# Add and GELU of two 1024 x 4096 arrays: one DMA queue, x kept in place, the additions on GpSimd, temporaries in PSUM

## The chip, the cores and the metric

The kernel runs on one core of a Trainium2 chip. The metric is the device time of one execution in microseconds (us). Before the change the median of three runs is 132.72 us (132.6 to 132.73). A profile of one execution, taken by the hardware profiler, goes with it; all times inside the kernel are from that one execution and count from the start of its span.

The engines in the profile are DVE (VectorE), ACT (ScalarE), POOL (GpSimd) and SP (SyncE), which here only issues transfers. SPq and POOLq are the instruction queues of SP and POOL. PE, the matrix engine, is not used.

## The reference

```
x, y: float32 [1024, 4096]
z = x + y
out = 0.5 * z * (1 + tanh(sqrt(2/pi) * (z + 0.044715 * z**3)))      # float32
```

Every element is independent of the others. 33.55 MB are read and 16.78 MB written.

## The kernel before

Each of the 128 partitions holds 8 whole rows of the arrays, that is 32768 consecutive floats or 128 KB of HBM. The kernel walks along these 32768 columns in 20 tiles: 15 of 2048 columns (8 KB per partition, 1 MB per transfer), and then a tail of 1024, 512, 256, 128 and 128 columns. Within a transfer the pieces of two neighbouring partitions lie 128 KB apart in HBM.

A tile goes through seven steps. `do_load` (L67, L68) issues two loads on SP's queue, x into a tile `a` and y into a tile `b`. `do_add` (L75) forms z = a + b on DVE. `do_sq` (L81) writes w = (sqrt_k3 * z)^2 on ACT. `do_stt` (L90) makes w = (w + k1) * z on DVE, which is the argument of the tanh. `do_ti` runs Tanh (L100) and then Identity with scale 0.5 and bias 0.5 (L105) on ACT. `do_mul_store` multiplies z by w on DVE (L116) and issues the store on POOL's queue (L117). So DVE has three passes over the data and ACT three.

All tiles lie in SBUF: six buffers each for `a` and `b`, five each for `z` and `w`. The order of the work is written out as a software pipeline, and each engine executes its instructions in the order in which they are written:

```
for t in range(C + 4):
    do_load(t); do_ti(t - 3); do_add(t - 1); do_stt(t - 2); do_sq(t - 1); do_mul_store(t - 3)
```

Waits between engines, and between a transfer and its users, are put in by the framework from the tiles that an instruction reads and writes.

Of the kernel before, what the change touches and what calls it, by code (L numbers as in the profile page):

```python
# [1 line left out]

# [1 line left out]

# [4 lines left out]


@with_exitstack
def kernel(
    ctx: ExitStack,
    tc: tile.TileContext,
    x: bass.AP,
    y: bass.AP,
    out: bass.AP,
):
    nc = tc.nc  # L20
    P = nc.NUM_PARTITIONS
    fp32 = mybir.dt.float32

    N, D = x.shape
    assert N % P == 0
    rows_per_part = N // P

    k1 = math.sqrt(2.0 / math.pi)
    k3 = k1 * 0.044715
    sqrt_k3 = math.sqrt(k3)  # L30

    xv = x.rearrange("(p n) d -> p (n d)", p=P)
    yv = y.rearrange("(p n) d -> p (n d)", p=P)
    ov = out.rearrange("(p n) d -> p (n d)", p=P)

    total_free = rows_per_part * D
    FMAX = 2048

    tail = [1024, 512, 256, 128, 128]
    nbody = (total_free - sum(tail)) // FMAX  # L40
    assert sum(tail) + nbody * FMAX == total_free
    sizes = [FMAX] * nbody + tail
    offsets = []
    off = 0
    for F in sizes:
        offsets.append(off)
        off += F
    C = len(sizes)

    in_pool = ctx.enter_context(tc.tile_pool(name="inputs", bufs=6))  # L50
    chain_pool = ctx.enter_context(tc.tile_pool(name="chain", bufs=5))
    consts = ctx.enter_context(tc.tile_pool(name="consts", bufs=1))

    half = consts.tile([P, 1], fp32, tag="half")
    nc.vector.memset(half, 0.5)  # L55

    a_t: list = [None] * C
    b_t: list = [None] * C
    z_t: list = [None] * C
    w_t: list = [None] * C  # L60

    def do_load(c):
        F = sizes[c]
        sl = slice(offsets[c], offsets[c] + F)
        a = in_pool.tile([P, F], fp32, tag="a")
        b = in_pool.tile([P, F], fp32, tag="b")
        nc.sync.dma_start(out=a, in_=xv[:, sl])  # L67
        nc.sync.dma_start(out=b, in_=yv[:, sl])  # L68
        a_t[c] = a
        b_t[c] = b  # L70

    def do_add(c):
        F = sizes[c]
        z = chain_pool.tile([P, F], fp32, tag="z")
        nc.vector.tensor_add(out=z, in0=a_t[c], in1=b_t[c])  # L75
        z_t[c] = z

    def do_sq(c):
        F = sizes[c]
        w = chain_pool.tile([P, F], fp32, tag="w")  # L80
        nc.scalar.activation(  # L81
            out=w,
            in_=z_t[c],
            func=mybir.ActivationFunctionType.Square,
            scale=sqrt_k3,
        )
        w_t[c] = w

    def do_stt(c):
        nc.vector.scalar_tensor_tensor(  # L90
            out=w_t[c],
            in0=w_t[c],
            scalar=k1,
            in1=z_t[c],
            op0=mybir.AluOpType.add,
            op1=mybir.AluOpType.mult,
        )

    def do_ti(c):
        nc.scalar.activation(  # L100
            out=w_t[c],
            in_=w_t[c],
            func=mybir.ActivationFunctionType.Tanh,
        )
        nc.scalar.activation(  # L105
            out=w_t[c],
            in_=w_t[c],
            func=mybir.ActivationFunctionType.Identity,
            scale=0.5,
            bias=half,  # L110
        )

    def do_mul_store(c):
        F = sizes[c]
        sl = slice(offsets[c], offsets[c] + F)
        nc.vector.tensor_mul(out=w_t[c], in0=z_t[c], in1=w_t[c])  # L116
        nc.gpsimd.dma_start(out=ov[:, sl], in_=w_t[c])  # L117

    for t in range(C + 4):
        if 0 <= t < C:  # L120
            do_load(t)
        if 0 <= t - 3 < C:
            do_ti(t - 3)
        if 0 <= t - 1 < C:
            do_add(t - 1)
        if 0 <= t - 2 < C:
            do_stt(t - 2)
        if 0 <= t - 1 < C:
            do_sq(t - 1)
        if 0 <= t - 3 < C:  # L130
            do_mul_store(t - 3)


# [1 line left out]
_INS = ['x', 'y']  # L135
_OUTS = [((1024, 4096), 'float32')]


# [23 lines left out]
```

## Time and profile before

| | before |
|---|---|
| median of 3 runs | 132.72 us |
| span of the profiled execution | 130.8 us (the median lies 1.9 us above it) |
| DVE busy | 107.8 us, 82% of the span, 61 instructions |
| ACT busy | 96.0 us, 73%, 61 instructions |
| POOL busy | 11.0 us, 8%, 24 instructions, nearly all of it issuing stores |
| read / written | 33.55 MB / 16.78 MB, 385 GB/s over the span |

How to read the lines that follow. The page cuts the span into 40 equal slices of 3.27 us; a digit is the busy share of a slice in tenths, and 9 means 90% or more. The line "DMA" is the mean busy share of the core's 16 DMA engines and "GB/s" what they moved. In the view by stretches each row gives a stretch, its length, the busy time of each engine with the number of instructions begun, PE's granted clock, the DMA engines' share and the rate. In the view by groups a row gives line, engine, operation, output and inputs with their shapes, the count, the busy time in us and the mean of one in ns, and the idle time of the engine just before them with what ended it. In the view by order of time a row gives the start, the duration, engine, line and operation, and in brackets the idle time before it and who ended it.

### The profile page before, as it was taken

The page shows a single profiled execution, that of the slowest core. Times are in us where ns is not written, and L with a number is a line of the kernel's source. Part 1 is how long each engine was busy: PE and PEld are TensorE (multiplying, and loading weights), DVE is VectorE, ACT ScalarE, POOL GpSimd, SP SyncE. Part 2 cuts the span into 40 slices and gives each one's busy share as a digit, 9 for nine tenths or more (in the row PEclk, how much of TensorE's full clock was granted, in tenths as well). Part 3 has the DMA queues.
Part 4 walks back from the last instruction along what each step waited for, and adds up shares of the span by engine and source line. Part 5 has one row for each costly group of instructions (what it writes and reads, how often), then busy time and mean ns, then how long its engine had stood idle before and what let it go on. Part 6 is the DMA issues. An engine that isn't in the chain of part 4 may idle for free.

```text
span 130.8 us, 306 instructions
## 1 busy us (share of the span) xinstructions
DVE 107.8 (82%) x61; ACT 96.0 (73%) x61; POOL 11.0 (8%) x24
## 2 busy tenths in 40 slices
DVE  0053949999999999988959899998969799999930
ACT  3005492899998989895975979885975959899850
POOL 0000002001000000101010100101010100110341
DMA  4999999999999999999999999999999999717690
GB/s 140 428 421 431 431 416 428 341 423 416 439 426 418 436 429 418 436 428 418 436 426 421 436 423 423 434 426 421 436 426 421 417 414 389 310 53 321 271 342 29
DMA packets 8258, 50.35 MB, mean 385 GB/s; under 512 B 960, under 2 KB 1728, under 8 KB 2496
## 3 DMA queue, kind: packets, MB, share of 16 engines
q1 hardware_dynamic: 5760, 33.56, 62.1%
q0 software_dynamic: 2496, 16.78, 30.9%
q14 instruction: 2, 0.02, 0.0%
HBM read 33.55 MB, written 16.78 MB: 385 GB/s over the span
## 4 chain that ended last, share of the span: by engine, by line
DMA 44%; issue 43%; POOL 5%; DVE 3%; POOLq 1%; SPq 0%; DVEq 0%
DMA b<-in_y_dram 44%; POOL out_dram L117 5%; DVE w L90 2%; DVE w L116 2%; POOLq L157 0%; SPq L67 0%; POOLq L117 0%; DVE z L75 0%; DVEq L75 0%
## 5 line engine op out<-in xcount | busy, mean ns | idle before, releaser
L75 DVE TENSOR_TENSOR z<-a,b 128x2048 f32<-128x2048 f32 (+4 forms) x20 | 37.2, 1862 | 13.1 <-DMA b<-in_y_dram 13.1
L81 ACT ACTIVATE w<-z 128x2048 f32<-128x2048 f32 (+4 forms) x20 | 31.3, 1563 | 22.5 <-DVE z L75 22.1
L116 DVE TENSOR_TENSOR w<-z,w 128x2048 f32<-128x2048 f32 (+4 forms) x20 | 37.2, 1860 | 3.0 <-ACT w L105 3.0
L90 DVE SCALAR_TENSOR_TENSOR w<-w,z 128x2048 f32<-128x2048 f32 (+4 forms) x20 | 37.1, 1859 | 2.4 <-ACT w L81 2.4
L100 ACT ACTIVATE w<-w 128x2048 f32<-128x2048 f32 (+4 forms) x20 | 31.3, 1566 | 7.0 <-DVE w L90 6.9
L105 ACT ACTIVATE w<-w,half 128x2048 f32<-128x2048 f32 (+4 forms) x20 | 33.2, 1659 | 0.6
L117 POOL DMA_DIRECT2D out_dram<-w x20 | 10.8, 541 | 116.6 <-DVE w L116 114.7
L81 ACT ACT_TABLE_LOAD x1 | 1.3, 1283 | 0.7 <-PEq L146 0.7
L55 DVE MEMSET half<- 128x1 f32 x1 | 0.1, 59 | 0.8 <-PEq L146 0.8
L146 POOL MEMSET const-float32-0.0<- 128x1 f32 x1 | 0.1, 98 | 0.2 <-issue 0.2
L146 POOL MEMSET const-bfloat16-1.0<- 128x1 bf16 x1 | 0.1, 101 | 0.0
L146 POOL MEMSET const-float32-1.0<- 128x1 f32 x1 | 0.1, 98 | 0.0
L146 POOL MEMSET const-uint8-127<- 128x1 uint8 x1 | 0.1, 98 | 0.0
## 6 DMA issues: line engine op xcount, KB each, us to landing
a<-in_x_dram SPq DMA_DIRECT2D x15, 1024.0 KB, 27.4
b<-in_y_dram SPq DMA_DIRECT2D x15, 1024.0 KB, 28.2
out_dram<-w POOLq DMA_DIRECT2D x15, 1024.0 KB, 9.1
a<-in_x_dram SPq DMA_DIRECT2D x1, 512.0 KB, 28.7
b<-in_y_dram SPq DMA_DIRECT2D x1, 512.0 KB, 26.3
out_dram<-w POOLq DMA_DIRECT2D x1, 512.0 KB, 3.8
a<-in_x_dram SPq DMA_DIRECT2D x1, 256.0 KB, 23.2
b<-in_y_dram SPq DMA_DIRECT2D x1, 256.0 KB, 21.4
```

The lines of the kernel that those rows point to most:

```text
L55: nc.vector.memset(half, 0.5)
L75: nc.vector.tensor_add(out=z, in0=a_t[c], in1=b_t[c])
L81: nc.scalar.activation(out=w, in_=z_t[c], func=mybir.ActivationFunctionType.Square, scale=sqrt_k3,)
L90: nc.vector.scalar_tensor_tensor(out=w_t[c], in0=w_t[c], scalar=k1, in1=z_t[c], op0=mybir.AluOpType.add, op1=mybir.AluOpType.mult,)
L100: nc.scalar.activation(out=w_t[c], in_=w_t[c], func=mybir.ActivationFunctionType.Tanh,)
L105: nc.scalar.activation(out=w_t[c], in_=w_t[c], func=mybir.ActivationFunctionType.Identity, scale=0.5, bias=half,)
L116: nc.vector.tensor_mul(out=w_t[c], in0=z_t[c], in1=w_t[c])
L117: nc.gpsimd.dma_start(out=ov[:, sl], in_=w_t[c])
L146: nc = _bacc.Bacc("TRN2", target_bir_lowering=False, num_devices=1)
```

## The change

The tiling changes first. There are 13 tiles, of 1024, 1024, 2048, six times 4096, 2048, 1024, 512 and 512 columns; a partition still reads and writes its own 128 KB, in pieces of up to 16 KB. Each tile of x has an SBUF buffer of its own, so x is resident as a whole (128 KB per partition). y has four buffers of 4096 columns, shared by the smaller tiles of one block. z is written over x, and the result over z, so the store goes out of x's buffer.

Computation goes in 33 chunks of at most 1024 columns. `add` runs on GpSimd for chunks 2 to 30 and on DVE for the first two and the last two. The temporary `w` lies in PSUM, in four buffers of 1024 columns. The function is written with a sigmoid, z * sigmoid(c1 * z + c1 * 0.044715 * z^3), which is the same function; the Identity pass of ACT goes away. One Sigmoid on a single column (`one`) is executed first.

All loads and all stores are issued by SP, on one queue. `LEAD` = 8192 sets their order: the store of a tile stands behind the loads that reach 8192 columns beyond the tile's end. The order on each engine is written out in four lists (`sp`, `pool`, `dve`, `acts`); `needs` and the last loop only interleave these lists in program order so that each instruction is written after those it depends on.

```diff
-    tail = [1024, 512, 256, 128, 128]
-    sizes = [FMAX] * nbody + tail
+    LEAD = 8192
+    CH = 1024
+    YB = 4
+    sizes = [1024, 1024, 2048] + [D] * (NB - 2) + [2048, 1024, 512, 512]
+    starts = [sum(sizes[:t]) for t in range(len(sizes))]
+    T = len(sizes)
...
+    chunks = []
+    for t in range(T):
+        o = 0
+        while o < sizes[t]:
+            f = min(CH, sizes[t] - o)
+            chunks.append((t, o, f))
+            o += f
+    C = len(chunks)
+    last = {t: c for c, (t, _, _) in enumerate(chunks)}
+    by_pool = set(range(2, C - 2))
-    in_pool = ctx.enter_context(tc.tile_pool(name="inputs", bufs=6))
-    chain_pool = ctx.enter_context(tc.tile_pool(name="chain", bufs=5))
+    xpool = ctx.enter_context(tc.tile_pool(name="xz", bufs=1))
+    ypool = ctx.enter_context(tc.tile_pool(name="y", bufs=YB))
+    ppool = ctx.enter_context(
+        tc.tile_pool(name="w", bufs=4, space=bass.MemoryType.PSUM)
+    )
...
+    def load_x(t):
+        xt[t] = xpool.tile([P, sizes[t]], fp32, tag=f"x{t}", name=f"x{t}")
+        nc.sync.dma_start(out=xt[t], in_=hbm(x, t))
+    def load_y(t):
+        n, o = divmod(starts[t], D)
+        if o == 0:
+            yb[n] = ypool.tile([P, D], fp32, tag="y", name=f"y{n}")
+        yt[t] = yb[n][:, o : o + sizes[t]]
+        nc.sync.dma_start(out=yt[t], in_=hbm(y, t))
+    def store(t):
+        nc.sync.dma_start(out=hbm(out, t), in_=xt[t])
+    def z(c):
+        t, o, f = chunks[c]
+        return xt[t][:, o : o + f]
-        nc.vector.tensor_add(out=z, in0=a_t[c], in1=b_t[c])
+    def add(c):
+        t, o, f = chunks[c]
+        eng = nc.gpsimd if c in by_pool else nc.vector
+        eng.tensor_add(out=z(c), in0=z(c), in1=yt[t][:, o : o + f])
+    def sq(c):
+        f = chunks[c][2]
+        wt[c] = ppool.tile([P, CH], fp32, tag="w", name=f"w{c}")[:, :f]
+        nc.scalar.activation(out=wt[c], in_=z(c), func=act.Square, scale=root)
+    def stt(c):
         nc.vector.scalar_tensor_tensor(
-            out=w_t[c], in0=w_t[c], scalar=k1, in1=z_t[c], op0=add, op1=mult
+            out=wt[c], in0=wt[c], scalar=c1, in1=z(c), op0=alu.add, op1=alu.mult
         )
-        nc.scalar.activation(out=w_t[c], in_=w_t[c], func=Tanh)
-        nc.scalar.activation(out=w_t[c], in_=w_t[c], func=Identity, scale=0.5, bias=half)
+    def sig(c):
+        nc.scalar.activation(out=wt[c], in_=wt[c], func=act.Sigmoid)
-        nc.vector.tensor_mul(out=w_t[c], in0=z_t[c], in1=w_t[c])
-        nc.gpsimd.dma_start(out=ov[:, sl], in_=w_t[c])
+    def mul(c):
+        nc.vector.tensor_mul(out=z(c), in0=wt[c], in1=z(c))
...
+    for t in range(T):
+        sp += [(load_x, t), (load_y, t)]
+        while s < T and starts[s] + sizes[s] + LEAD <= starts[t] + sizes[t]:
+            sp.append((store, s))
+            s += 1
+    sp += [(store, t) for t in range(s, T)]
+    for c in range(C):
+        if c in by_pool:
+            pool.append((add, c))
+    for i in range(-3, C + 1):
+        if 0 <= i < C:
+            dve.append((stt, i))
+            acts.append((sig, i))
+        if 0 <= i - 1 < C:
+            dve.append((mul, i - 1))
+        if 0 <= i + 3 < C and i + 3 not in by_pool:
+            dve.append((add, i + 3))
+        if 0 <= i + 2 < C:
+            acts.append((sq, i + 2))
...
+        one = xpool.tile([P, 1], fp32, tag="one", name="one")
+        nc.vector.memset(one, 0.0)
+        nc.scalar.activation(out=one, in_=one, func=act.Sigmoid)
```

More of the change, by code (lines that the diff above doesn't have):

```diff
@@ L22 @@
     fp32 = mybir.dt.float32
+    act = mybir.ActivationFunctionType
+    alu = mybir.AluOpType
     N, D = x.shape
     assert N % P == 0
[L26 to L37, printed above, removed]
-    tail = [1024, 512, 256, 128, 128]
-    nbody = (total_free - sum(tail)) // FMAX
@@ L41 @@
-    assert sum(tail) + nbody * FMAX == total_free
-    sizes = [FMAX] * nbody + tail
[L43 to L48, printed above, removed]
-    in_pool = ctx.enter_context(tc.tile_pool(name="inputs", bufs=6))
-    chain_pool = ctx.enter_context(tc.tile_pool(name="chain", bufs=5))
[L52 to L85, printed above, removed]
-        )
[L87 to L131, printed above, removed]
+    NB = N // P
+    TOT = NB * D
+    c1 = 2.0 * math.sqrt(2.0 / math.pi)
+    root = math.sqrt(c1 * 0.044715)
+    LEAD = 8192
+    CH = 1024
@@ new lines, with hbm @@
+    YB = 4
+    sizes = [1024, 1024, 2048] + [D] * (NB - 2) + [2048, 1024, 512, 512]
+    assert sum(sizes) == TOT
+    starts = [sum(sizes[:t]) for t in range(len(sizes))]
+    T = len(sizes)
+    def hbm(ap, t):
+        v = ap.rearrange("(p n) d -> p (n d)", p=P)
+        return v[:, starts[t] : starts[t] + sizes[t]]
+    chunks = []
[5 more added lines that the diff above has]
+            o += f
@@ new lines, in sq @@
+    def sq(c):
[3 more added lines that the diff above has]
+    def stt(c):
+        nc.vector.scalar_tensor_tensor(
+            out=wt[c], in0=wt[c], scalar=c1, in1=z(c), op0=alu.add, op1=alu.mult
+        )
+    def sig(c):
+        nc.scalar.activation(out=wt[c], in_=wt[c], func=act.Sigmoid)
+    def mul(c):
+        nc.vector.tensor_mul(out=z(c), in0=wt[c], in1=z(c))
@@ new lines @@
+    needs = {
+        load_x: lambda t: [],
+        load_y: lambda t: [
+            (add, c)
+            for c, (i, _, _) in enumerate(chunks)
+            if starts[t] % D == 0 and starts[i] // D == starts[t] // D - YB
+        ],
+        add: lambda c: [(load_y, chunks[c][0]), (load_x, chunks[c][0])],
+        sq: lambda c: [(add, c)] + ([(mul, c - 4)] if c >= 4 else []),
+        stt: lambda c: [(sq, c)],
+        sig: lambda c: [(stt, c)],
+        mul: lambda c: [(sig, c)],
+        store: lambda t: [(mul, last[t])],
+    }
@@ new lines @@
+    queues = [sp, pool, acts, dve]
+    done = set()
+    with tc.manual_schedule():
+        one = xpool.tile([P, 1], fp32, tag="one", name="one")
+        nc.vector.memset(one, 0.0)
+        nc.scalar.activation(out=one, in_=one, func=act.Sigmoid)
+        while any(queues):
+            moved = False
+            for q in queues:
+                while q and all(n in done for n in needs[q[0][0]](q[0][1])):
+                    fn, arg = q.pop(0)
+                    fn(arg)
+                    done.add((fn, arg))
+                    moved = True
+                    if q is not sp:
+                        break
+            assert moved, [q[:1] for q in queues]
```

3 lines of the change are left out of this document (added).

## The prediction

> **What bounds the kernel now.** I read the page first: busy shares, the slices, the bytes.
>
> ```profile
> span 130.8 us, 306 instructions
> DVE 107.8 (82%) x61; ACT 96.0 (73%) x61; POOL 11.0 (8%) x24
> ...
> DMA  4999999999999999999999999999999999717690
> GB/s 140 428 421 431 431 416 428 341 423 416 439 426 418 436 429 418 436 428 418 436 426 421 436 423 423 434 426 421 436 426 421 417 414 389 310 53 321 271 342 29
> ...
> HBM read 33.55 MB, written 16.78 MB: 385 GB/s over the span
> ```
>
> The DMA digits are 9 from the second slice to the 34th, at about 425 GB/s, and then fall apart: one slice moves 53 GB/s. So the transfers set the pace for some 110 us, and in the last 20 us they wait for something. The next view is the busy time by stretch, with the DMA engines' share and rate.
>
> ```profile
> core 0: us, DVE busy (x) ACT busy (x) POOL busy (x), PEclk, DMA share, GB/s
> 0.00:2.00 2.00, 0.06 (x1) 1.27 (x1) 0.20 (x4) 1.00 0.17 37
> 2.00:3.00 1.00, 0.00 (x0) 0.02 (x1) 0.00 (x0) 1.00 0.84 270
> 3.00:4.00 1.00, 0.00 (x0) 0.00 (x0) 0.00 (x0) 1.00 1.03 426
> ...
> 60.00:80.00 20.00, 18.07 (x9) 14.48 (x9) 1.06 (x2) 1.00 1.01 428
> ...
> 110.00:114.00 4.00, 4.00 (x3) 3.73 (x3) 0.53 (x1) 1.00 0.79 295
> 114.00:118.00 4.00, 4.00 (x4) 3.56 (x2) 0.53 (x1) 1.00 0.28 113
> 118.00:122.00 4.00, 4.00 (x5) 3.68 (x6) 0.53 (x1) 1.00 0.61 250
> 122.00:126.00 4.00, 3.14 (x9) 3.06 (x9) 2.09 (x4) 1.00 0.93 374
> 126.00:131.00 5.00, 0.29 (x1) 0.69 (x2) 0.60 (x2) 1.00 0.34 120
> ```
>
> Loads and stores together run at 428 GB/s with a DMA share of 1.01: full. From 110 on DVE is busy for 12 us without a break while the DMA share drops to 0.28. DVE works off its backlog, and the stores wait. The order of instructions there:
>
> ```profile
> 116.87 0.53 POOL L117 DMA_DIRECT2D out_dram<-w  x1 [5.01 <-DVE w L116]
> ...
> 118.56 2.28 DVE L116 TENSOR_TENSOR w<-z,w 128x2048 f32<-128x2048 f32 x1
> ...
> 121.14 0.53 POOL L117 DMA_DIRECT2D out_dram<-w  x1 [3.74 <-DVE w L116]
> ```
>
> POOL, which issues the stores, waits 5.0 and 3.7 us for DVE's last multiplication. At 428 GB/s the 50.33 MB need 117.6 us; the span is 13.2 us longer. That is 2.2 us at the start (0 to 4 us move 74 + 270 + 426 KB = 0.77 MB, which is 1.8 us of full rate, so the stream starts in effect at 2.2), some 2 us after the last byte, and about 9 us of holes, nearly all behind 110.
>
> **The change, part by part.** The bytes stay, so the floor of 117.6 us stays. What can go is the holes.
>
> *Compute per 1024 columns.* The rows by shape:
>
> ```profile
> L75 DVE TENSOR_TENSOR z<-a,b 128x1024 f32<-128x1024 f32 x1 | 1.2, 1218 | 0.0
> L90 DVE SCALAR_TENSOR_TENSOR w<-w,z 128x1024 f32<-128x1024 f32 x1 | 1.2, 1218 | 0.0
> L81 ACT ACTIVATE w<-z 128x1024 f32<-128x1024 f32 x1 | 1.0, 1042 | 0.0
> L105 ACT ACTIVATE w<-w,half 128x1024 f32<-128x1024 f32 x1 | 1.1, 1132 | 0.0
> ...
> L75 DVE TENSOR_TENSOR z<-a,b 128x512 f32<-128x512 f32 x1 | 0.7, 686 | 0.0
> L81 ACT ACTIVATE w<-z 128x512 f32<-128x512 f32 x1 | 0.6, 612 | 0.0
> L81 ACT ACT_TABLE_LOAD x1 | 1.3, 1283 | 0.7 <-PEq L146 0.7
> ```
>
> The Identity pass goes (1.13 us per chunk), Sigmoid takes Tanh's place at Tanh's price, so ACT needs 2 x 1.04 = 2.08 us a chunk. Its one table load is called forth early by the activation on `one`, as now at 0.7 us, in the shade of the first load. DVE keeps two operations, 2 x 1.22 = 2.44 us a chunk, plus the adds of four chunks. Three streams of 512 KB a chunk are 1.573 MB, 3.67 us at 428 GB/s. Both engines have a third of their time to spare, so no backlog like that of now can build up.
>
> *PSUM operands.* The trace has none. The bound below is the SBUF row, 1.22; above, an operand at half speed makes 2.44 an operation, which would be 4.88 a chunk and more than the DMA's 3.67. I take 1.22 plus up to 0.1: nothing about a dense float row suggests a second pass over it. [...]
>
> *The add on GpSimd.* No row shows POOL computing a tile. Below stands DVE's row, 1.22. Above I put 3.66, DVE's price three times over, as for an engine that does its two reads and its write one after another. Between them I take 2.44, two reads after each other. Twenty-nine adds are 71 us beside a 118 us stream, 2.44 against 3.67 a chunk, so hidden. [...]
>
> *Stores on SP's queue.* POOL's 20 store issues go; SP now issues 26 loads and 13 stores in order. A store that waits for its multiplication holds every load behind it, and, as the next rows show, SP is held by another thing too.
>
> ```profile
> 4.17 0.45 SPq L68 DMA_DIRECT2D b<-in_y_dram  x1
> 5.60 0.33 SPq L67 DMA_DIRECT2D a<-in_x_dram  x1
> 8.06 0.33 SPq L68 DMA_DIRECT2D b<-in_y_dram  x1
> ```
>
> Twelve buffers are free, yet after eight issues the ninth waits, and the next come 2.46 us apart, one per landing: eight transfers may be outstanding on a queue. In the changed kernel eight are mostly 2 MB each, over 30 us of work, so that limit costs nothing. Does a store starve the stream? In the middle, store t-2 stands behind the loads of tile t. Its last multiplication comes on DVE after the next tile's first `stt`, and `sig` of that chunk comes on ACT after the next tile's first `sq`, so it waits for tile t-1 to land, then add, square, `stt`, multiplication: 1.0 + 2.44 + 1.04 + 1.22 + 1.22 = 6.9 us (the 1.0 is from the first tile: 2 MB from 2.2 on are through at 7.1, its add starts at 8.14). Behind tile t-1's landing the queue still holds store t-3 and tile t's loads, 14.7 us. That is 7.8 us of cover for one wait of SP. At the head, tile 3 lands at 22.8 (8.4 MB, 19.6 us, and 1.0 after 2.2), store 2 is ready 5.9 later at 28.7, and the loads ahead of it last until 31.6; stores 0 and 1 add 2.5. Cost nothing; without that cover it would be its lateness, microsecond for microsecond.
>
> *The tail.* Call E the moment the last load's data are through. Behind it stand stores 7 to 12, 6.3 MB or 14.7 us, under which the last chunks must be computed. Store 9 must start at E+9.8, so be issued by E+8.5 (first issue at 0.74, data from about 2.0: 1.3 us ahead). Tile 8's data are through at E-14.7 (store 6 and 4096 columns of loads follow), so by the prices above POOL's adds of it run from E-13.7 to E-3.9 and end for chunks 28 to 30 at E-1.5, 1.0 and 3.4; `stt` 28 is done at E+0.8 (1.04 + 1.22 later), and DVE runs without a gap from E+0.8 (mul 27, add 31, stt 29, mul 28, add 32, stt 30, mul 29: 5 x 1.22 + 2 x 0.69 = 7.5) to E+8.3. That is just in time; the last store is ready at E+12.2 against E+12.8. With up to 0.1 more for each PSUM operation a hole of up to 0.9 opens. I take 0.4.
>
> *Rate of the stream.* Every partition's rows lie 128 KB apart before and after; a row grows from 8 to 16 KB. Stores alone also run full, and the last bytes end like this:
>
> ```profile
> 118.00:119.00 1.00, 1.00 (x3) 1.00 (x3) 0.00 (x0) 1.00 1.03 426
> 119.00:120.00 1.00, 1.00 (x1) 1.00 (x2) 0.00 (x0) 1.00 1.05 426
> ...
> 127.00:128.00 1.00, 0.05 (x1) 0.00 (x0) 0.54 (x1) 1.00 0.56 193
> 128.00:129.00 1.00, 0.00 (x0) 0.00 (x0) 0.00 (x0) 1.00 0.19 66
> ```
>
> Loads alone 426 (3 to 4 us), both 428, stores alone 426: one queue in order should keep 428. Bounds: 421 (the poorer full slices), 119.5 us, and 436 (the better ones), 115.4 us. After the last byte, between 128.2 and 129, the span lasts 1.8 to 2.6 us; I take 2.3.
>
> **Sum.** 2.2 + 117.6 + 0.4 + 2.3 = 122.5 us of span. The median of the runs, 132.72, is 1.9 above the profiled span of 130.8, so 124.4 us, 8.3 less than before.
>
> **The rivals.**
>
> 1. *A hole in the tail.* If the add costs 3.0, POOL ends chunk 30 at E+7.3 instead of 3.4 (seven adds from E-13.7), store 9 is ready at E+10.8, 2.3 late, and later ones with it: about 127. For it: the tail has 0.2 us to spare. Against it: only a price in the upper half of the bounds does this.
>
> 2. *POOL and DVE exclude each other: slower.* If DVE's operations cannot run while POOL adds, a chunk costs 2.44 + 2.44 = 4.88 us, more than the DMA's 3.67. From tile 3's landing at 22.8 on, 27 chunks take 131.8, and some 10 us follow (square, two multiplications, short chunks, last stores, end): 164.6, or 166.5 us. It decides from 3.3 us a chunk on, and from 3.63 on the change is slower. The present POOL row of 11.0 us, all issues, tells neither way. [...]
>
> 3. *The change doesn't fill the stream.* No row shows stores issued by SP, or read and written bytes in turn on one queue. For no change the 50.33 MB would have to take 125.8 us; with loads at 428 (78.4) the stores would run at 354 GB/s. Then 132.7. Against it: 426 for each alone.
>
> 4. *Square and Sigmoid in different tables.* Some 66 loads of 1.28 are 85 us more on ACT, 153 in all: over 160 us. Now three functions share one load.
>
> **How the numbers follow.** Forecast 0.72, its own range 122.6 (433 GB/s, so 116.2, and no hole) to 126.3 (421 GB/s, so 119.5). Rival 1: 0.14, at 126 to 128.5. Rival 2: 0.06. Rival 3: 0.05, spread over 129 to 135. Rival 4: 0.02; 0.01 for none of these. The range 122.6 to 128.2 leaves out rivals 2 to 4 and the ends. A change within 0.2% is what a measurement can't tell from none; it has 0.02 of rival 3. Slower: rivals 2 and 4 and some of 3, 0.09; faster 0.89.
>
> **What would show it.** Right: the DMA digits stay at 9 up to the last two slices, about 428 GB/s with no slice like 53; POOL's add at 2 to 2.6 us; DVE near 82 us and ACT near 68 busy, with waits; the chain ends in stores of `out_dram` on SP's queue. Rival 1 shows as a hole in the slices after the loads end, with SP waiting for DVE; rival 2 as `stt` or adds far longer than 1.3 and 2.5 us; rival 3 as slices near 350 while only stores flow; rival 4 as a table load per activation. I am wrong if the stream has holes between 35 and 100 us, for which I found no cause.

## The result, and the profile after

The changed kernel takes 125.96 us (median of 4 runs, 125.25 to 126.61) against 132.7 us before. The ratio is 0.9491 with a 95% interval of 0.9456 to 0.9526, so it is about 5% faster. The forecast was 124.4 us with a range of 122.6 to 128.2. The profiled execution has a span of 124.8 us; its own time is 126.61, the slowest of the four, so 1.8 us lie around the span, about as before (1.9).

The page of the changed kernel, the parts that answer to those shown of before:

```profile
span 124.8 us, 301 instructions
DVE 79.1 (63%) x71; ACT 64.2 (51%) x68; POOL 67.4 (54%) x33
...
DMA  4999999999899999999999999999999999999494
GB/s 88 417 437 452 433 431 420 425 420 420 345 461 433 425 415 415 431 441 431 425 425 441 420 425 431 441 436 425 425 412 410 417 415 411 450 420 425 184 392 165
```

The digits of the DMA engines now stay at 9 up to the 37th slice, but for one 8 in the 11th (345 GB/s, at 31 to 34 us, where the queue passes to the first stores), and only one slice late in the span is poor (184 GB/s; before, five slices lay between 53 and 342). No compute engine is busy for more than 63%. DVE has lost all but four of its additions: 79.1 us in place of 107.8.

The groups by shape, whose durations the prediction had to guess or carry over:

```profile
L92 POOL TENSOR_TENSOR x<-x,y 128x1024 f32<-128x1024 f32 x29 | 67.2, 2346 | 43.7 <-DMA y<-in_y_dram 43.7
L100 DVE SCALAR_TENSOR_TENSOR w<-w,x 128x1024 f32<-128x1024 f32 x31 | 38.1, 1231 | 34.3 <-ACT w L97 34.3
L108 DVE TENSOR_TENSOR x<-w,x 128x1024 f32<-128x1024 f32 x31 | 37.6, 1213 | 0.0
L97 ACT ACTIVATE w<-x 128x1024 f32<-128x1024 f32 x31 | 31.9, 1028 | 51.5 <-POOL x L92 45.1 <-DVE x L92 6.4
L105 ACT ACTIVATE w<-w 128x1024 f32<-128x1024 f32 x31 | 30.5, 983 | 2.1 <-DVE w L100 2.0
```

An addition on POOL takes 2.346 us. An operand in PSUM changes DVE by +13 and -6 ns against the 1218 and 1219 ns from SBUF, and ACT by -14 and -57 ns against 1042 and 1040 (the last of these was a Tanh, so that the function changed too). POOL idles 43.7 us waiting for loads: it is far from being the bound.

The poor slice, in stretches of 1 us, and the last microseconds of the transfers:

```profile
core 0: us, DVE busy (x) ACT busy (x) POOL busy (x), PEclk, DMA share, GB/s
115.00:116.00 1.00, 1.00 (x2) 0.14 (x1) 0.00 (x0) 1.00 0.70 295
116.00:117.00 1.00, 1.00 (x2) 1.00 (x2) 0.00 (x0) 1.00 0.19 82
117.00:118.00 1.00, 1.00 (x2) 0.79 (x2) 0.00 (x0) 1.00 0.37 156
118.00:119.00 1.00, 1.00 (x2) 0.17 (x1) 0.00 (x0) 1.00 0.92 385
...
122.00:123.00 1.00, 0.00 (x0) 0.00 (x0) 0.00 (x0) 1.00 0.98 371
123.00:124.00 1.00, 0.00 (x0) 0.00 (x0) 0.00 (x0) 1.00 0.05 18
```

Here is the hole that the prediction was afraid of. About 1.8 us of full work are missing between 115 and 118 (0.31 + 0.81 + 0.64), and DVE is busy throughout. The order of time in this place, and the wait of SP's queue that belongs to it:

```profile
94.48 9.26 POOL L92 TENSOR_TENSOR x<-x,y 128x1024 f32<-128x1024 f32 x4 [6.21 <-DMA y<-in_y_dram]
...
110.02 1.80 DVE L92 TENSOR_TENSOR x<-x,y 128x512 f32<-128x512 f32 x1
...
114.01 0.67 DVE L92 TENSOR_TENSOR x<-x,y 128x512 f32<-128x512 f32 x1
...
116.98 0.33 SPq L83 DMA_DIRECT2D out_dram<-x  x1
```

```profile
SPq L83 <- DVE x L108: 86.0, 12, 14.1
```

Store 9 is issued at 116.98, when DVE has multiplied; the engines have run out of work at about 115.5. SP waits 86 us in all for DVE, but only this wait leaves the engines idle.

**What the hole hides.** The trace has 16 landing records for each transfer, as many as the core has DMA engines; I take them as one part per engine. First and last part, in us from the start of the span, read from these records:

```
transfer        changed kernel          lead_all (below)
                first  last   apart     apart
y of tile 3      22.5   23.1   0.60     0.50
y of tile 5      47.4   48.7   1.33     0.50
y of tile 8      91.3   94.3   3.07     0.52
store 8         116.2  119.0   2.80     1.28
store 9         120.7  121.5   0.80     1.29
```

In the changed kernel one or two of the 16 parts come ever later than the others, until the last is 3 us behind, and the users of a transfer wait for its last part (below, POOL starts on tile 8 at 94.48). At the hole the first parts pause for 4.4 us between stores 8 and 9, but the last parts follow each other by 2.45 us, which is what 1 MB needs at 428 GB/s. So the engine that comes last does not seem to idle in the hole at all. From this reading came the two theories of the first experiments.

### The profile page after: what moved, and what is told of

Its sections match the earlier page's. It is cut to its first block, busy times and chain, and to the rows that moved or that the text cites. A ratio compares the mean times of both kernels' runs of the same rounds, so it can differ in the third digit from the quotient of the medians.

```text
span 124.8 us, 301 instructions
## 1 busy us (share of the span) xinstructions
DVE 79.1 (63%) x71; ACT 64.2 (51%) x68; POOL 67.4 (54%) x33
## 3 DMA queue, kind: packets, MB, share of 16 engines
q1 hardware_dynamic: 5616, 50.33, 96.7%
## 4 chain that ended last, share of the span: by engine, by line
DMA 64%; POOL 15%; DVE 11%; SPq 3%; ACT 2%; issue 2%; POOLq 0%
DMA y<-in_y_dram 64%; POOL x L92 15%; DVE x L108 5%; DVE w L100 5%; SPq L73 2%; ACT w L97 2%; DVE x L92 1%; SPq L80 1%; ACT w L105 0%; SPq L83 0%; POOLq L92 0%
## 5 line engine op out<-in xcount | busy, mean ns | idle before, releaser
L92 POOL TENSOR_TENSOR x<-x,y 128x1024 f32<-128x1024 f32 x29 | 67.2, 2346 | 43.7 <-DMA y<-in_y_dram 43.7
L100 DVE SCALAR_TENSOR_TENSOR w<-w,x 128x1024 f32<-128x1024 f32 (+1 forms) x33 | 39.5, 1198 | 34.3 <-ACT w L97 34.3
L97 ACT ACTIVATE w<-x 128x1024 f32<-128x1024 f32 (+1 forms) x33 | 33.1, 1002 | 51.5 <-POOL x L92 45.1
L108 DVE TENSOR_TENSOR x<-w,x 128x1024 f32<-128x1024 f32 (+1 forms) x33 | 39.0, 1181 | 0.1
L105 ACT ACTIVATE w<-w 128x1024 f32<-128x1024 f32 (+1 forms) x33 | 31.6, 958 | 3.5 <-DVE w L100 3.4
L92 DVE TENSOR_TENSOR x<-x,y 128x1024 f32<-128x1024 f32 (+1 forms) x4 | 4.9, 1231 | 6.3 <-DMA y<-in_y_dram 6.3
```

Source lines behind the costliest of these rows:

```text
L92: eng.tensor_add(out=z(c), in0=z(c), in1=yt[t][:, o : o + f])
L97: nc.scalar.activation(out=wt[c], in_=z(c), func=act.Square, scale=root)
L100: nc.vector.scalar_tensor_tensor(out=wt[c], in0=wt[c], scalar=c1, in1=z(c), op0=alu.add, op1=alu.mult)
L105: nc.scalar.activation(out=wt[c], in_=wt[c], func=act.Sigmoid)
L108: nc.vector.tensor_mul(out=z(c), in0=wt[c], in1=z(c))
```

## The experiments

**The changed kernel again**, as a measure for the others.

> The changed kernel as it is, timed in more rounds beside the ones below. In its profile the body of the stream took some 1.5 us more than forecast, and there is a hole: between 115.5 and 118 us the DMA engines are mostly idle, because store 9 (L83) is issued only at 116.98. Expected: 125.25 to 126.6 us as in its first four runs, median about 126.0. Its spread of 1.1% is itself a question: before the change four runs lay within 0.1%.

Measured: 125.68 us in five runs (124.84 to 126.65), ratio 0.9477 (0.943 to 0.9523); a sixth took 126.8. Differences below are against this 125.68. The spread is there again, 1.6% over all six. The kernels below with all loads ahead of all stores lie within 0.2 to 0.4 us, but so do the four runs of lead_12288, which has five turns (0.42).

**The stream without arithmetic.** `add`, `sq`, `stt`, `sig` and `mul` are left out, so the output is x itself. The wait of a load of y for the additions that free its buffer goes with them.

```diff
...
-        store: lambda t: [(mul, last[t])],
+        store: lambda t: [(load_x, t)],
-    queues = [sp, pool, acts, dve]
+    queues = [sp]
```

> All arithmetic is left out; the 26 loads and 13 stores go out on SP's queue in the same order, a store waits for its load of x alone. So this is the stream without any lateness of the compute. Theory A (the hole costs its length): the time falls by the 1.5 us of the hole, to 124.4. Theory B (the hole is hidden, because one of the 16 DMA engines lags: by the landing records of the changed kernel's profile the last of a transfer's 16 parts comes 0.6 us after the first at 24 us, but 3.0 us after it at 108 us, and on the last engine store 9 follows store 8 by 2.44 us, which is its bare transfer time): the time falls by at most 0.4 us, to 125.6 or more. If the stream were as forecast, 428 GB/s without a lag, it would be 2.2 + 117.6 + 1.8 + 1.8 = 123.4.

Measured: 125.7 us (124.73 to 126.16). The stream alone takes as long as the whole kernel, the same at the medians within a spread of over 1 us. Its profiled execution is the fastest of the four, 124.73:

```profile
GB/s 87 417 432 432 434 426 437 432 426 400 339 440 448 426 442 426 426 426 426 426 426 426 426 426 426 426 426 426 426 426 426 400 424 405 440 432 432 408 411 183
```

The hole is not there, and the time is not 1.5 us lower at the median, as theory A would have it. Theory B holds: the compute, and the hole with it, costs next to nothing.

**More cover for the tail.**

```diff
-    LEAD = 8192
+    LEAD = 12288
```

> LEAD = 12288 in place of 8192: one more tile of stores (4096 columns, 4.9 us) is kept for the time after the last load. The compute is then ahead of the last stores by about 2 us more than it was late (2.5 us). Theory A: no hole, 1.5 us faster, 124.4 to 124.6. Theory B: no hole either, but no gain, 125.6 to 126.2, since the engine that comes last did not idle in the hole.

Measured: 126.41 us (126.01 to 126.43). The slices of its page:

```profile
DMA  4999999999999999999999999999999999999991
GB/s 85 419 434 455 431 431 426 421 421 431 421 421 431 387 434 421 431 426 373 421 442 436 405 426 431 436 431 400 421 408 421 405 444 427 421 431 442 408 367 41
```

The hole is gone, and the time is not better: with transfers_only, this shows that the hole cost nothing. The landings say why: of the last store the first part now lands at 121.18 us in place of 123.29, but the last part at 123.74 in place of 123.92. The poor places now are single slices at 387, 373, 405 and 400 GB/s, the 14th, 19th, 23rd and 28th, some 15 us apart. The records of single packets say more. Of the 16 KB packets, which take 0.611 us in the median, the ones that took over 0.1 us longer:

```
changed kernel             lead_12288
around   count  worst      around   count  worst
31 us     20    +0.58      40.5 us   10    +0.37
46 us      8    +0.83      56 us     26    +0.70
61 us      3    +0.76      71 us     11    +0.66
76 us      2    +0.26      85 us     11    +1.00
90 us      4    +0.89      others     3    +0.41
others     2    +0.44
```

Each group named by a time lies where the queue passes from the loads of a tile to a store, and with LEAD larger by a tile the groups have moved with these places (the first store stands 9.8 us later).

**One turn only.**

```diff
-    LEAD = 8192
+    LEAD = 32768
```

> LEAD = 32768: all loads first, then all stores; the queue turns from loads to stores once instead of six times. In the changed kernel's trace some engines' packets are long by up to 0.9 us at about 31, 46, 61, 76 and 90 us, each where the queue passes from loads of a tile to a store. Theory B1 (each such turn costs the lagging engine something, about 2.5 us over the kernel): 123.2 to 124.0, and the lag between first and last part of a transfer stays under 1.5 us. Theory B2 (the stalls come with each store's first touch of its columns, wherever it stands in the queue, or with something else): about 126, as now. Theory A: 124.4 to 124.6, by the missing hole alone.

Measured: 124.66 us (124.56 to 124.75), ratio 0.9394 (0.9376 to 0.9413).

```profile
DMA  3999999999999999999999999999999999999993
GB/s 84 415 438 430 438 427 427 427 427 427 427 432 432 427 438 427 427 427 427 427 427 427 427 408 411 396 405 435 448 432 427 438 432 427 427 432 427 414 412 119
```

With all loads first the loads run at 427 GB/s slice after slice, no 16 KB packet after the first 5 us is longer than usual by 0.1 us, the parts stay within 0.55 us of each other up to the turn at about 76 us and within 1.35 behind it, and the runs lie within 0.2 us. It is 1.0 us faster than the changed kernel beside it (1.36 with the sixth run counted, as an expectation below has it). This lies just above A's numbers and above B1's, and well below B2's. A is excluded by lead_12288, and B2 by the stores themselves, which touch the same columns here without a long 16 KB packet. What is left is B1 at a smaller price than its 2.5 us: the passing from loads to stores in one queue.

The profiles say how far this goes. The first and the last part of a transfer are at most 3.15 us apart in the profiled execution of the changed kernel (126.61 us), 2.6 in that of lead_12288 (126.43), 2.2 in that of same_again (125.68) and 0.8 in that of transfers_only (124.73). So the time goes with the late part; but six turns do not leave a part behind in every execution, and the one in which they did not took as long as lead_all. The slower executions of transfers_only have no trace. Whether the arithmetic has a share in the late part is therefore not shown.

**Is it a price per turn?** Without arithmetic again, with 16 equal tiles, once with 12 turns and once with one.

```diff
-    sizes = [1024, 1024, 2048] + [D] * (NB - 2) + [2048, 1024, 512, 512]
+    sizes = [2048] * 16          # turns_12: LEAD = 8192; turns_1: LEAD = 32768
```

> No arithmetic, as in transfers_only, but 16 equal tiles of 2048 columns with LEAD = 8192: the queue turns from loads to stores 12 times, with 2 MB of loads and 1 MB of stores between turns, in place of 6 times. Theory T (a turn inside one queue costs the engine that comes last about 0.27 us: lead_all with one turn was 1.36 us faster than the changed kernel with six): turns_1 plus 11 x 0.27 = 3.0 us. Theory M (the cost goes by the amount moved between turns, or is something else than the turn): at most 1.4 us over turns_1, as between the changed kernel and lead_all.

> The same 16 tiles of 2048 columns without arithmetic, all loads ahead of all stores: one turn. The control of turns_12. Packets of 8 KB take 309 ns, those of 16 KB 612 ns, so 0.6 us more than lead_all's in the body: 124.4 to 125.3 in either theory.

Measured: turns_1 124.40 us (124.26 to 124.58), turns_12 125.13 us (124.56 to 125.81). Twelve turns cost 0.7 us and not 3.0. That is no more than six turns with twice the amount between them: 1.0 us with the arithmetic, and 1.0 without it if lead_all stands for the one turn there (125.7 - 124.66). Theory T with a fixed price per turn falls. Two of the four runs of turns_12 took 124.6, as with one turn, and two 125.7 and 125.8; the profile is of a fast one (124.58), and its parts stay within 0.75 us. So the alternation costs 0.7 to 1.0 us at the median, in some executions over 1 and in others next to nothing; what in it does, and why not in proportion, stays open.

**The rows of a transfer 16 KB apart in place of 128 KB.**

```diff
-        v = ap.rearrange("(p n) d -> p (n d)", p=P)
-        return v[:, starts[t] : starts[t] + sizes[t]]
+        n, o = divmod(starts[t], D)
+        return ap[n * P : (n + 1) * P, o : o + sizes[t]]
```

> Another assignment of rows to partitions: partition p takes row n*128 + p for block n, so the rows of one transfer lie 16 KB apart in HBM (one 2 MB piece) in place of 128 KB apart. LEAD is 8192 as in the changed kernel, and all else is the same. Theory P (the stalls at the turns from loads to stores come of the rows' distance of 128 KB): no long packets at 46, 61, 76 and 90 us, 124.2 to 124.8 with a spread of a few tenths. Theory T (the turn itself stalls the engines, wherever the rows lie): 125.4 to 126.8, as the changed kernel.

> The rows of a transfer 16 KB apart as in rows_near, and all loads ahead of all stores (LEAD = 32768). It tells how much the distance of rows costs where there is one turn only. lead_all at 128 KB measured 124.66. Theory P: 124.3 to 124.7, at most 0.3 less, since there the loads already ran at 427 GB/s without a stall. Theory T: the same 124.5 to 124.8.

Measured: rows_near 128.09 us (127.51 to 128.69), near_lead_all 125.81 us (125.5 to 125.86). Neither theory had this: it is slower by 2.4 and 1.15 us. The slices of rows_near:

```profile
GB/s 112 247 387 431 439 436 436 426 436 426 393 432 400 426 379 368 436 426 431 431 426 441 431 426 426 420 431 436 431 418 420 418 413 397 457 420 441 252 393 160
```

The loss that both share is at the head, where the pieces are 4 and 8 KB: 247 and 387 GB/s in the second and third slice against 417 and 437. That is some 0.63 MB or 1.5 us less by 9.5 us (slices of 3.16 and 3.12 us). The dips at the turns are there as well (379 and 368), long packets too, and the last part is up to 2.9 us behind. So the distance of 128 KB is not what stalls the turns, and the small pieces at the head were better off with it; why is not shown.

**Stores on a second queue.**

```diff
-        nc.sync.dma_start(out=hbm(out, t), in_=xt[t])
+        nc.scalar.dma_start(out=hbm(out, t), in_=xt[t])
-        while s < T and starts[s] + sizes[s] + LEAD <= starts[t] + sizes[t]:
-            sp.append((store, s))
-            s += 1
-    sp += [(store, t) for t in range(s, T)]
...
+        acts += [(store, t) for t in range(T) if last[t] == i - 3]
+    acts += [(store, t) for t in range(T) if last[t] > C - 3]
```

> The single queue is undone: the 13 stores are issued on ACT's queue, each three steps of ACT's list behind its last multiplication, so loads and stores go on two queues and a store waits behind no load. Rows 128 KB apart. Theory T (turns within one queue stall; packets in turn from two queues, as in the kernel before, do not): no long packets after the first store. But stores now go out early and the loads end late: with 12.6 MB stored by then the last load is through at about 110 and tile 8 lands at about 96.5; some 25 us of add, ACT and DVE work follow it (so it was in the changed kernel: 94.5 to 119.9), then 3.5 us for the last store and the end, so 125 to 126 of span, 127 to 128 in time. If the single queue brought nothing: 126.0.

Measured: 126.79 us (126.44 to 127.38), ratio 0.9555 (0.9536 to 0.9574).

```profile
GB/s 83 419 437 449 433 423 423 433 417 407 434 410 428 398 425 443 430 449 423 417 428 423 449 449 423 417 420 438 417 423 416 449 429 420 423 94 334 376 412 214
```

The stream runs without a lead and then has a real hole (94 GB/s): the last tiles' compute is no longer covered by stores kept back. This hole holds up the last part as well: the last parts of stores 7 and 8 land 7.4 us apart, where 2 MB need 4.9. Groups of long packets stand only at 30 and 43 us. They are not a matter of one queue alone: in the kernel before, with its two queues, 42 packets of 8 KB were long by over 0.1 us (worst +0.61 on 0.309) at 23.8 to 27.8 us, while its first store was under way. The single queue with its lead brings 1.1 us; the edit takes back both at once, and by the hole what they bring lies in the tail, in the stores kept back for it. The time is a little under the 127 to 128 expected.

**Temporaries in SBUF.**

```diff
-        tc.tile_pool(name="w", bufs=4, space=bass.MemoryType.PSUM)
+        tc.tile_pool(name="w", bufs=3)
...
-        sq: lambda c: [(add, c)] + ([(mul, c - 4)] if c >= 4 else []),
+        sq: lambda c: [(add, c)] + ([(mul, c - 3)] if c >= 3 else []),
```

> The temporaries in SBUF in place of PSUM (three buffers of 1024 columns, since a fourth has no room). scalar_tensor_tensor and the multiplication then have both inputs in SBUF. Rival 2 of the prediction (POOL and DVE exclude each other) would now hold for every one of them: 2.35 + 2.44 = 4.8 us a chunk, 155 to 168 us, with POOL's add or DVE's operations far over 2.35 and 1.22. The other theory, that DVE and POOL run side by side whatever memory w lies in, and PSUM brings nothing: 126 to 128 us. The one DVE add that overlapped a POOL add in the changed kernel's tail (512 columns, 1.80 us in place of 0.68) speaks for the first.

Measured: 153.76 us, ratio 1.1599 (1.1578 to 1.162). The groups by shape, and a stretch in order of time:

```profile
L92 POOL TENSOR_TENSOR x<-x,y 128x1024 f32<-128x1024 f32 x29 | 87.9, 3062 | 40.4 <-DMA y<-in_y_dram 40.4
L100 DVE SCALAR_TENSOR_TENSOR w<-w,x 128x1024 f32<-128x1024 f32 x31 | 64.4, 2077 | 11.6 <-ACT w L97 11.6
L108 DVE TENSOR_TENSOR x<-w,x 128x1024 f32<-128x1024 f32 x31 | 63.4, 2045 | 0.0
```

```profile
44.16 3.32 POOL L92 TENSOR_TENSOR x<-x,y 128x1024 f32<-128x1024 f32 x1
45.20 3.36 DVE L100 SCALAR_TENSOR_TENSOR w<-w,x 128x1024 f32<-128x1024 f32 x1
...
48.03 12.59 POOL L92 TENSOR_TENSOR x<-x,y 128x1024 f32<-128x1024 f32 x4 [0.55 <-DMA y<-in_y_dram]
48.48 3.37 DVE L108 TENSOR_TENSOR x<-w,x 128x1024 f32<-128x1024 f32 x1
...
62.77 1.21 DVE L100 SCALAR_TENSOR_TENSOR w<-w,x 128x1024 f32<-128x1024 f32 x1
```

While POOL adds, a DVE operation takes 3.36 us and an addition about 3.3: in 3.3 us one of each gets done, nearly the time of one after the other (1.21 + 2.35 = 3.56). When POOL rests, DVE is back at 1.21. So the two nearly exclude each other, once both inputs of DVE's operation lie in SBUF. It is the inputs: the multiplication writes to SBUF in either kernel, and takes 1.21 us with one input in PSUM. The three buffers in place of four can't do this: the operations themselves are longer. The time is a little under the 155 forecast because POOL's additions don't cover all of DVE's operations: their means of 2.08 and 2.05 us lie between 1.21 and 3.36.

**The additions back on DVE.**

```diff
-    by_pool = set(range(2, C - 2))
+    by_pool = set()
```

> GpSimd's additions undone: all 33 adds on DVE, all else as in the changed kernel. DVE then has 3 x 1.22 = 3.67 us a chunk (the pitch of back-to-back operations in the changed kernel's trace is 1.13, so 3.4), which is as much as the three streams need, 3.67. Theory D (DVE becomes a bound as strong as the stream and its waits at tile borders are no longer made up): 129 to 134 us, DVE over 115 us busy. Theory S (the stream alone sets the time as long as DVE's pitch is under it): 126 to 127.5.

Measured: 135.21 us (134.63 to 136.0), ratio 1.0195 (1.0145 to 1.0244): about 2% slower than the kernel before. The additions by group, and the time by stretches:

```profile
L92 DVE TENSOR_TENSOR x<-x,y 128x1024 f32<-128x1024 f32 (+1 forms) x33 | 39.0, 1182 | 19.5 <-DMA y<-in_y_dram 19.5
```

```profile
80.00:100.00 20.00, 17.45 (x16) 9.99 (x11) 0.00 (x0) 1.00 1.00 415
100.00:120.00 20.00, 20.00 (x19) 11.27 (x13) 0.00 (x0) 1.00 0.71 291
120.00:134.00 14.00, 9.97 (x12) 5.68 (x8) 0.00 (x0) 1.00 0.73 300
```

That is the end of the kernel before once more: DVE without a break, the DMA engines waiting. Theory D was right in kind; its 129 to 134 us were 1.2 too low at the upper end, and its mark of 115 us of DVE was too high. DVE is busy for 109.7 us and waits 19.5 for loads, since it can't start a tile of 4096 columns before it has landed; these waits it does not make up.

**A version that is faster.** The experiments say what matters: one turn, and no small pieces.

```diff
-    sizes = [1024, 1024, 2048] + [D] * (NB - 2) + [2048, 1024, 512, 512]
+    sizes = [D] * NB
-    LEAD = 8192
+    LEAD = 32768
```

> All loads ahead of all stores, and 8 equal tiles of 4096 columns in place of 13: with 39 us of stores behind the last load nothing needs small tiles at the end, and at the head compute is not what the end waits for. Both theories of the turns expect the same; the question is what the small transfers cost. In lead_all the stretch around the turn, with its small pieces, moves 396 to 411 GB/s for four slices (about 0.6 us lost), and the first packets of 4 KB take up to 0.9 us more than their share. Expected: 123.6 to 124.4, against 124.66; if small pieces cost nothing: 124.6.

Measured: 123.62 us (123.5 to 123.67), ratio 0.9316 (0.9301 to 0.9331), 1.0 us less than lead_all, from which only the sizes differ, and 2.1 less than the changed kernel.

```profile
span 121.8 us, 271 instructions
...
GB/s 102 430 430 430 430 430 430 430 430 430 430 430 430 430 430 430 420 430 425 430 430 430 430 430 428 422 430 430 430 430 430 430 430 430 430 430 430 430 430 102
```

From the second slice to the last but one it moves 420 to 430 GB/s. Little is left but the start, the end and the bytes.

## Why the prediction was right, and where not

**The bound.** Right: the transfers set the time, and the holes of before go. transfers_only at 125.7 shows it without any arithmetic, and adds_on_dve at 135.2 shows that it takes the additions on POOL for the holes of before to go.

**The sum.** The span was to be 2.2 + 117.6 + 0.4 + 2.3 = 122.5. In the profiled execution the bytes up to 4 us (37 x 2 + 156 + 422 KB = 0.65 MB, 1.5 us) put the start at 2.5; the last bytes are through at about 123.05 (single packets of 2 KB follow, the last until 123.57), so the end takes 1.75; between lie 120.55 us in place of 118.0. The start and the end were off by +0.3 and -0.55. The term that was mis-sized is the stream: "one queue in order should keep 428". All rows that this rested on were of loads alone, stores alone, or both on two queues. In one queue, loads and stores in turn left the last of a transfer's 16 parts up to 3 us late in this execution, and the time is that of the last part. 50.33 MB in 120.55 us are 417 GB/s, a little below the 421 that I gave as the lower bound. This is the slowest of the four runs; for the median, 0.65 us shorter, the same reckoning gives an estimate of 420. The median stayed under the 126.3 that goes with 421 all the same, because the end was 0.55 us shorter than taken and the 0.4 for the hole did not come on top of the stream. That was luck. With one turn and no small pieces the stream is what the sum said: 430 GB/s, 123.62 us, 0.8 below the forecast.

**The tail.** It was sized at 0.4 us with 0.2 to spare, and the hole came out at 1.8 us of idle engines, beside two things that the profile shows: tile 8 was added from 94.48 on, when its last part had landed at 94.3, 3 us after its first; and one of DVE's additions took 1.80 in place of 0.67 us, while POOL was adding (until 111.27). But that a hole in the mean rate costs its length, by which the 0.4 stands in the sum, was a wrong step: lead_12288 removes the hole and gains nothing, because its last part lands at nearly the same time (123.74 against 123.92). The idle engines and the late part are not to be added; what the alternation costs is the 1.0 us by which lead_all is faster, in which the hole is gone as well.

**The prices.** POOL's addition was taken at 2.44, an estimate between two bounds, and measured 2.346. A PSUM operand was taken at up to 0.1 us an operation, an estimate as well; the rows show 13 ns at most. DVE was forecast at about 82 us and measured 79.1, ACT at 68 and 64.2.

**The waits of SP.** SP never had more than eight transfers outstanding: five of its issues (at 5.80, 88.60, 94.36, 99.23 and 101.73) came 0.01 to 0.07 us after a landing, with seven others under way. That cost nothing, as said: the DMA digits are at 9 in those slices. Store 2 was to be ready at 28.7 and is issued at 29.04. SP stands 86.0 us at stores in all, and up to the tail the digits stay at 9 but for the 11th slice, which is as poor without arithmetic (339 GB/s in transfers_only): costed at nothing, and rightly. The chain of the page was to end in stores on SP's queue; as the trace has it, it ends in DVE's last multiplication, from 119.93 to 120.62, behind which only the last store is issued.

**The rivals.** Rival 1, a hole in the tail: it came, without the price of the add that I had made its condition, and it did not matter. Rival 2, POOL against DVE: in this kernel at one addition only, but real. Its 0.06 was an estimate; no row of before showed either way. With w in SBUF it costs 28 us. DVE's durations beside POOL go with where its inputs lie: 1.21 to 1.23 us with one input in PSUM (this kernel), 3.36 with both in SBUF (w_in_sbuf), and 1.80 for this kernel's 512-column addition at 110.02, also with both in SBUF. That is 1.1 us more than the 0.67 of the addition at 114.01, when POOL was done. Rival 3, a stream that one queue doesn't fill: its mechanism was nearest to what happened, at a far smaller price: the median lies 1.6 us above the forecast, where rival 3 had 8.3. Rival 4: one table load of 1.28 us, so no.

## What to carry to other kernels

Before moving an elementwise operation to GpSimd, look where the inputs of what DVE does meanwhile lie. Here, with one of them in PSUM, the move was worth 9.5 us (additions back on DVE: 135.2); with both in SBUF the kernel takes 153.8, 21 us more than the kernel before. In a kernel that transfers set, first run the transfers without arithmetic: if that takes as long, as here (125.7 us against 125.68), the order of the transfers is the thing to try. Here the order was worth 1.0 us (lead_all), and closing the hole by itself nothing (lead_12288, 126.41). Where all inputs fit, try to load everything, then store everything, in the largest pieces: here 123.6 us.

## What the runs showed that was not expected

- Where one queue passed from loads to stores, single packets took up to 1.0 us longer than their 0.61, and the last of 16 parts fell up to 3 us behind, though not in every execution. At the median it costs 0.7 to 1.0 us, and the runs differ more: 124.84 to 126.8 us with six turns, 124.56 to 124.75 with one. It is not a price per turn (12 turns: 0.7 us).
- A visible hole of 1.8 us, with SP waiting for DVE, cost nothing: the part that came last did not pause there, which the mean over 16 DMA engines does not show.
- With pieces of 4 and 8 KB at the head, rows 16 KB apart in HBM ran at 247 GB/s where rows 128 KB apart ran at 417.
